# Modulation sums of a hybrid decoder block: two steps leave TensorE, four steps are joined in pairs

## The chip, the cores and the metric

The kernel runs on one core of one Trainium2 chip. The metric is the device time of one launch in microseconds (us), the median of three runs. The engines are named as the profile names them: PE is TensorE's stream of products (PEld its weight loads), DVE is VectorE, ACT is ScalarE, POOL is GpSimd, and SP is the queue that issues every DMA of this kernel.

## The reference

One decoder layer over 512 tokens of width 1024, all in float32. A conditioning vector c gives six modulation vectors; two of them (shift1 and scale1) shape the input of the token mixer, whose first product is one wide projection w_in:

```
c_act = jax.nn.silu(c)
mod = c_act @ w_ada[l] + b_ada[l]
shift1, scale1, gate1, shift2, scale2, gate2 = [m[:, None, :] for m in jnp.split(mod, 6, axis=-1)]
h = rms_norm(x, g_pre_mix[l]) * (1.0 + scale1) + shift1
y = token_mixer(h, ...)          # h @ w_in, then GLU and convolution, latent attention, gates
x = x + gate1 * rms_norm(y, g_post_mix[l])
h = rms_norm(x, g_pre_mlp[l]) * (1.0 + scale2) + shift2
y = jnp.square(jax.nn.relu(h @ w_mlp_in[l])) @ w_mlp_out[l]
x = x + gate2 * rms_norm(y, g_post_mlp[l])
```

In the mixer, the first 2048 columns of `h @ w_in` go through a GLU and a causal depthwise convolution of 31 taps over 1024 channels, the next 704 columns are the latents of the attention, and the last 2048 are gates.

## The kernel before

Every float32 product is made as three products of split operands: a matrix is split into a rounded high part (ACT casts it) and the rest (DVE subtracts), and PE adds high times high, high times low and low times high. So each weight that is loaded costs one ACT cast and one DVE subtraction before PE may use it. Tiles lie in two large SBUF arenas, `f_arena` (float32) and `r_arena` (the split parts), so nearly all operations carry one of these two names, and the line of a helper (L410) that issues them.

The kernel is written as a list of operations. A planner (class `Planner`) gives each one an estimated cost and a due time, and lays out the order of every engine's queue from them (`plan`, L327 on). It keeps a model of the DMA rings with one time at which they come free (`dma_free`, L341), and it repeats the plan up to 14 times with other places in the arenas and keeps the one that it reckons shortest. Engines then run their queues strictly in order. A change of any cost or of the list can therefore move work anywhere in the program.

The opening is the part that the change touches. The model width is cut in eight steps k of 128 channels. A step needs the shift and the scale of its 128 channels: `ada_load` brings 128 or more columns of w_ada (eight row blocks j, 4 DMAs of 256 KB for one step), `g1_load` brings 448 KB of w_in, and the sum over c's 1024 entries is made. `to_columns` (L657) turns the sums into columns, one channel to a partition, by products with `ones`, and adds the bias into the tile `mod`. `first_products` (L669) then makes the modulated h of the step (ACT writes the high part, DVE the low part), splits the step's w_in weights and issues 21 products of 128 x 512 into seven PSUM banks that collect all eight steps. In the prediction "the 168 products" are these 8 x 21.

How the sum over c is made depends on the step. For k = 0 and 1 (L689 to L713) PE makes it: 8 products of the column `cT` with the weights into one PSUM row, which ACT copies out. For k = 2 to 7 (L714 on, one step to a group of `KGRP`) DVE makes it on all partitions: one `tensor_scalar` and seven `scalar_tensor_tensor` on 256 columns, each reading the accumulator that the one ahead of it wrote, and the products with `ones` add up the partitions.

Ahead of the 168 products PE transposes the normalised x (32 transposes of 128 x 128); DVE and ACT copy them out. Behind them come the first GLU tiles, then the latent projection (its weights are the 128 x 704 splits on ACT and DVE), then the attention heads and, over a long stretch of DVE's queue, the convolution: 8 channel tiles with 31 steps of 128 x 512 each, 248 steps, two tiles in alternation. The convolution steps stand in DVE's queue between the splits and the softmax work that PE waits for.

Of the kernel before, what the change touches and what calls it, by code (L numbers as in the profile page):

```python
# [15 lines left out]
ALU = mybir.AluOpType  # L16

P = 128
# [3 lines left out]
KD = D // P  # L22
# [27 lines left out]
LEAD = 15000.0  # L50
SLOW = 4000.0
ADAS = (1, 1, 0, 4)
KGRP = ((2,), (3,), (4,), (5,), (6,), (7,))
HX, HA, HG, HC = 1.2e5, 1e5, 3e3, 1.1e5


# [113 lines left out]
class Planner:  # L170
# [154 lines left out]
    def plan(self):  # L325
        ops = self.ops
        pe_t = 0.0  # L327
        big = sum(o.cost for o in ops if o.eng == "pe") + TAIL
        for o in ops:
            o.dead = big  # L330
            if o.eng == "pe":
                pe_t += o.cost
                o.dead = pe_t
        for o in reversed(ops):
            lat = o.post + (2.0 * o.dma if o.dma else 0.0)
            for s in o.succ:
                q = ops[s]
                o.dead = min(o.dead, q.dead - q.cost - lat)
        heaps = {e: [] for e in self.NAMES}
        free = {e: 0.0 for e in self.NAMES}  # L340
        dma_free = 0.0  # L341
        landed = [0.0] * DEPTH
        future = []

        def key(o):
            return (o.rank, o.i) if o.eng == "pe" else (o.dead - o.hurry, o.i)

        for o in ops:
            o.ndep, o.ready = len(o.deps), 0.0
            if not o.ndep:  # L350
                heapq.heappush(future, (0.0, o.i))
        order = []
        now = 0.0
        while len(order) < len(ops):
            while future and future[0][0] <= now:
                o = ops[heapq.heappop(future)[1]]
                heapq.heappush(heaps[o.eng], (key(o), o.i))
            for e in self.NAMES:
                if free[e] <= now and heaps[e]:
                    o = ops[heapq.heappop(heaps[e])[1]]  # L360
                    o.t0 = now
                    free[e] = now + o.cost
                    if o.dma:
                        st = max(now + 1100.0, dma_free)
                        dma_free = st + o.dma
                        o.t1 = dma_free + 1100.0
                        landed.append(o.t1)
                        free[e] = max(free[e], landed[-DEPTH])
                    else:
                        o.t1 = free[e] + o.post  # L370
                    order.append(o)
                    for s in o.succ:
                        q = ops[s]
                        q.ndep -= 1
                        q.ready = max(q.ready, o.t1 if (q.eng != o.eng or o.dma) else free[e] if e == "pe" else max(free[e], o.t1 - 30))
                        if not q.ndep:
                            heapq.heappush(future, (q.ready, q.i))
            nxt = [free[e] for e in self.NAMES if free[e] > now and heaps[e]]
            if future:
                nxt.append(future[0][0])  # L380
            if not nxt:
                break
            now = max(now, min(nxt)) if min(nxt) > now else now
        assert len(order) == len(ops)
        self.length = max(o.t1 for o in ops)
        return order
# [28 lines left out]
def tile_hybrid_block(  # L415
# [34 lines left out]
    ones = const.tile([P, P], F32, name="ones")  # L450
# [13 lines left out]
    def emit(past, replay):  # L464
# [79 lines left out]
        def ada_load(ks):  # L544

            n = len(ks) * P
            b = fa.alloc(2 * KD * n)
            v = fa.v(b, "p (s j n) -> p s j n", j=KD, s=2)
            src = w_ada.rearrange("(j p) (s n) -> p s j n", p=P, s=6)
            step = KD // 2  # L550
            for j in range(0, KD, step):
                for s in range(2):
                    sp.dma_start(out=v[:, s, j:j + step], in_=src[:, s, j:j + step, ks[0] * P:ks[0] * P + n])
            return b, v
# [102 lines left out]
        def to_columns(src, lp, ks):  # L657

            for s in range(2):
                for i, k in enumerate(ks):  # L660
                    pe.matmul(pb.v(bg)[:, s * KD + k:s * KD + k + 1], lhsT=src[:, s, i * P:(i + 1) * P], rhs=ones[0:lp, 0:1],
                              start=True, stop=True)
            ksl = slice(ks[0], ks[-1] + 1)
            dve.tensor_tensor(mod[:, 0, ksl], pb.v(bg)[:, ksl], col("bada", ks[0], len(ks)), ALU.add)
            for k in ks:
                dve.scalar_tensor_tensor(mod[:, 1, k:k + 1], pb.v(bg)[:, KD + k:KD + k + 1], b1p[:, k:k + 1], col("gpm", k),
                                         op0=ALU.add, op1=ALU.mult)
# [17 lines left out]
                              stop=k == KD - 1 and wi == 1)  # L685
            w.free()


        plan.boost = 1000  # L689
        ad0 = [ada0]  # L690
        plan.hurry = HA - 1e4
        ad0.append(ada_load((1,)))
        wbs = []
        for k in range(2):
            plan.hurry = HA - (5e3 if k == 0 else 1.5e4)
            wbs.append(g1_load(k))
        plan.hurry = HG
        for k in range(2):
            av = ad0[k][1]
            ro = pb.v(bg)[0:1, 256:512].rearrange("p (s n) -> p s n", s=2)  # L700
            for j in range(KD):
                pe.matmul(ro, lhsT=cT[:, j:j + 1], rhs=av[:, :, j], start=j == 0, stop=j == KD - 1)
            fa.free(ad0[k][0])
            acc = fa.alloc(2 * P)
            accv = fa.v(acc, "p (s n) -> p s n", s=2)[0:1]
            act.copy(accv, ro)
            to_columns(accv, 1, (k,))
            fa.free(acc)
        plan.boost = 0
        plan.hurry = 0.0  # L710
        for k in range(2):
            first_products(k, wbs[k])

        for ks in KGRP:  # L714
            plan.hurry = HA - 1e4 * ks[0]
            n = len(ks) * P
            ab, av = ada_load(ks)
            ada_end = len(plan.ops) - 1
            plan.hurry -= 5e3
            wbs = [g1_load(k) for k in ks]  # L720
            plan.hurry = HG
            plan.boost = 1000
            acc = fa.alloc(2 * n)
            accv = fa.v(acc, "p (s n) -> p s n", s=2)
            for j in range(KD):
                if j == 0:
                    dve.tensor_scalar(accv, av[:, :, 0], cT[:, 0:1], None, ALU.mult)
                else:
                    dve.scalar_tensor_tensor(accv, av[:, :, j], cT[:, j:j + 1], accv, op0=ALU.mult, op1=ALU.add)
            fa.free(ab)  # L730
            to_columns(accv, P, ks)
            fa.free(acc)
            plan.boost = 0
            plan.hurry = 0.0
            for k, wb in zip(ks, wbs):
                first_products(k, wb)
# [1043 lines left out]
```

## Time and profile before

| what | time |
|---|---|
| median of three runs | 816.17 us (815.13 to 816.69) |
| the profiled execution | 815.82 us |
| its span, first to last instruction | 814.0 us |
| PE busy, DVE busy in the span | 796.5 us, 732.2 us |
| end of the 168 products | 66.2 us from the span's start |

The profiled execution lies 1.8 us above its own span and 0.35 us below the median. Times "at" a point are counted from the span's start. A busy PE in this profile is a modelled one, so stretches in which PE is all busy can hold short waits; the weight loads (PEld) show these better.

### The profile page before, as it was taken

Reading aid. Unit: us, or ns where it says so; the run is one execution under the profiler, and the core shown is the slowest. Engines: PE = TensorE matmul, PEld = TensorE weight load, DVE = VectorE, ACT = ScalarE, POOL = GpSimd, SP = SyncE. Lnnn points to the kernel's source line nnn. Section 1 sums busy time; section 2 is a strip of 40 time slices with the busy share of each in tenths; the row PEclk is TensorE's granted clock in tenths of the full one; section 3 lists DMA queues with packets and bytes.
Section 4 is the critical chain, followed back from the end, with each engine's and each line's share of the span. In section 5 each row is a group of like instructions: output and inputs, shape, how many; then the busy total and the mean of one; then the engine's idle time right before and its main releaser. Section 6 shows DMA issues by size and latency. Waiting matters only on the chain.

```text
span 814.0 us, 11293 instructions
## 1 busy us (share of the span) xinstructions
PE 796.5 (98%) x4222; PEld 681.1 (84%) x4222; DVE 732.2 (90%) x1049; ACT 441.6 (54%) x735; POOL 22.0 (3%) x77
## 2 busy tenths in 40 slices
PE   6999999999999999999999999999999999999996
PEld 3778988889897888878888889988998889888885
DVE  3898999999999999998899589899889989996696
ACT  5455453365885247237434387676665547554543
POOL 2001010000000000000000010000000000000001
PEclk9999999999999999999999999999999999999999
DMA  9989433112253250451799253026403580590302
GB/s 296 314 257 320 148 122 104 52 53 65 91 182 80 77 151 31 155 170 63 268 316 369 77 202 112 2 78 199 137 2 98 186 292 18 163 301 2 104 1 103
DMA packets 91337, 117.31 MB, mean 144 GB/s; under 512 B 7473, under 2 KB 66194, under 8 KB 91282
## 3 DMA queue, kind: packets, MB, share of 16 engines
q1 hardware_dynamic: 91282, 116.59, 44.9%
q8 instruction: 33, 0.54, 0.3%
q14 instruction: 22, 0.18, 0.1%
HBM read 108.18 MB, written 8.39 MB: 143 GB/s over the span
## 4 chain that ended last, share of the span: by engine, by line
PE 84%; DVE 8%; ACT 3%; DMA 2%; issue 1%; POOL 1%; SPq 0%; DVEq 0%
PE psum L410 84%; DVE f_arena L410 5%; DVE r_arena L410 3%; ACT f_arena L410 2%; ACT r_arena L410 1%; DMA c<-in_c_dram 1%; DMA f_arena<-in_w_in_dram 1%; POOL stats L410 1%; ACT stats L410 0%; SPq L410 0%; DMA rows<-in_kv_norm_g_dram 0%; DVE mod L410 0%; DVEq L1775 0%; DVEq L410 0%
## 5 line engine op out<-in xcount | busy, mean ns | idle before, releaser
L410 PE MATMUL psum<-r_arena 128*128 128x512 f32 (+3 forms) x3880 | 756.4, 355 | 0.9 <-ACT r_arena L410 0.6
L410 PEld LDWEIGHTS psum<-r_arena 128*128 128x128 f32 x3880 | 640.1, 189 | 100.7 <-ACT r_arena L410 2.6
L410 ACT CAST r_arena<-f_arena 128x1024 fp32r<-128x1024 f32 (+4 forms) x240 | 224.9, 964 | 169.1 <-PE psum L410 115.3
L410 DVE TENSOR_TENSOR r_arena<-f_arena,r_arena 128x1024 fp32r<-128x1024 f32 (+4 forms) x250 | 265.9, 1089 | 31.2 <-PE psum L410 21.4
L410 DVE SCALAR_TENSOR_TENSOR f_arena<-f_arena,cw 128x512 f32<-128x512 f32 x240 | 165.8, 738 | 0.0
L410 DVE TENSOR_TENSOR f_arena<-f_arena 128x1024 f32<-128x1024 f32 (+3 forms) x99 | 102.3, 1047 | 3.0 <-ACT r_arena L410 1.6
L410 ACT ACTIVATE f_arena<-f_arena 128x512 f32<-128x512 f32 (+4 forms) x112 | 66.1, 606 | 29.0 <-DVE f_arena L410 27.9
L410 ACT ACTIVATE f_arena<-psum 128x512 f32<-128x512 f32 x52 | 30.6, 594 | 71.9 <-PE psum L410 71.3
L410 DVE SCALAR_TENSOR_TENSOR f_arena<-f_arena,cT 128x256 f32<-128x256 f32 (+1 forms) x70 | 56.0, 801 | 7.4 <-DMA f_arena<-in_w_ada_dram 6.4
L410 DVE TENSOR_TENSOR f_arena<-psum,f_arena 128x512 f32<-128x512 f32 x64 | 42.9, 681 | 6.8 <-PE psum L410 6.8
L410 ACT COPY f_arena<-psum 128x512 f32<-128x512 f32 (+5 forms) x54 | 26.8, 517 | 33.2 <-PE psum L410 33.1
L410 PE MATMUL psum<-ident,f_arena 128*128 128x128 f32 x234 | 35.4, 291 | 8.2 <-DVE f_arena L410 8.1
L410 PEld LDWEIGHTS psum<-ident,f_arena 128*128 128x128 f32 x234 | 29.0, 149 | 14.1 <-DVE f_arena L410 9.3
L410 ACT CAST r_arena<-psum 128x512 fp32r<-128x512 f32 (+2 forms) x57 | 30.2, 563 | 12.1 <-PE psum L410 11.8
L410 DVE TENSOR_TENSOR r_arena<-psum,r_arena 128x512 fp32r<-128x512 f32 (+2 forms) x57 | 35.8, 654 | 0.6 <-ACT r_arena L410 0.3
L410 POOL TENSOR_TENSOR stats<-stats,nhalf 128x1 f32<-128x1 f32 (+1 forms) x17 | 13.3, 785 | 471.2 <-ACT stats L410 471.1
L410 ACT ACTIVATE r_arena<-f_arena 128x512 fp32r<-128x512 f32 (+3 forms) x20 | 13.0, 651 | 18.0 <-DVE f_arena L410 15.4
L410 ACT ACTIVATE r_arena<-f_arena,mod 128x512 fp32r<-128x512 f32 x8 | 6.5, 816 | 21.1 <-DVE mod L410 21.1
L410 DVE TENSOR_SCALAR f_arena<-f_arena,stats 128x1024 f32<-128x1024 f32 x8 | 6.0, 753 | 12.7 <-POOL stats L410 12.7
L410 DVE CUSTOM_DVE_ANT_0 f_arena<-psum,mask 128x128 f32<-128x128 f32 (+3 forms) x32 | 14.8, 481 | 0.1
L410 DVE SCALAR_TENSOR_TENSOR f_arena<-f_arena 128x512 f32<-128x512 f32 (+1 forms) x18 | 13.2, 740 | 0.0
L410 DVE SCALAR_TENSOR_TENSOR f_arena<-f_arena,psum 128x512 f32<-128x512 f32 x16 | 10.8, 678 | 2.2 <-ACT f_arena L410 2.2
(94 smaller groups left out, 182.9 us busy)
## 6 DMA issues: line engine op xcount, KB each, us to landing
f_arena<-in_w_ada_dram SPq DMA_DIRECT2D x16, 1024.0 KB
f_arena<-in_w_mlp_in_dram SPq DMA_DIRECT2D x32, 512.0 KB
f_arena<-in_w_mlp_out_dram SPq DMA_DIRECT2D x32, 512.0 KB
f_arena<-in_w_in_dram SPq DMA_DIRECT2D x24, 512.0 KB
f_arena<-in_w_ada_dram SPq DMA_DIRECT2D x32, 256.0 KB
f_arena<-in_x_dram SPq DMA_DIRECT2D x8, 512.0 KB
h_spill<-r_arena SPq DMA_DIRECT2D x16, 256.0 KB
f_arena<-in_w_attn_out_dram SPq DMA_DIRECT2D x8, 512.0 KB
```

The costliest lines, as they stand in the source:

```text
L410: getattr(self.real[o.eng], o.fn)(*o.a, **o.k)
```

## The change

- `KGRP` becomes `((0,), (1,), (2, 3), (4, 5), (6,), (7,))`: all eight steps go through the same loop, with steps 2 and 3 and steps 4 and 5 in one group each. A pair is loaded by 4 DMAs of 512 KB with rows of 1024 bytes (128 x 4 x 256), and summed by operations of 512 columns.
- The branch that made the sums of steps 0 and 1 on PE goes, with its two ACT copies.
- The sum on DVE has two accumulators, one for the even and one for the odd j: two `tensor_scalar` and six `scalar_tensor_tensor`, in alternation, so that an operation reads what the one before the last wrote.
- `to_columns` takes both accumulators: for each column of `mod` two products with `ones` that add up in PSUM, where there was one.
- The planner's DMA ring starts as free at 1500 in place of 0 (nanoseconds of its model).

```diff
-KGRP = ((2,), (3,), (4,), (5,), (6,), (7,))
+KGRP = ((0,), (1,), (2, 3), (4, 5), (6,), (7,))
...
-        dma_free = 0.0
+        dma_free = 1500.0
...
-                    pe.matmul(pb.v(bg)[:, s * KD + k:s * KD + k + 1], lhsT=src[:, s, i * P:(i + 1) * P], rhs=ones[0:lp, 0:1],
-                              start=True, stop=True)
+                    for q, a in enumerate(src):
+                        pe.matmul(pb.v(bg)[:, s * KD + k:s * KD + k + 1], lhsT=a[:, s, i * P:(i + 1) * P], rhs=ones[0:lp, 0:1],
+                                  start=q == 0, stop=q == len(src) - 1)
...
-        for k in range(2):
-            av = ad0[k][1]
-            ro = pb.v(bg)[0:1, 256:512].rearrange("p (s n) -> p s n", s=2)
-            for j in range(KD):
-                pe.matmul(ro, lhsT=cT[:, j:j + 1], rhs=av[:, :, j], start=j == 0, stop=j == KD - 1)
-            fa.free(ad0[k][0])
-            acc = fa.alloc(2 * P)
-            accv = fa.v(acc, "p (s n) -> p s n", s=2)[0:1]
-            act.copy(accv, ro)
-            to_columns(accv, 1, (k,))
-            fa.free(acc)
...
-            ab, av = ada_load(ks)
+            ab, av = ada0 if ks == (0,) else ada_load(ks)
...
-            acc = fa.alloc(2 * n)
-            accv = fa.v(acc, "p (s n) -> p s n", s=2)
+            acc = [fa.alloc(2 * n) for _ in range(2)]
+            accv = [fa.v(a, "p (s n) -> p s n", s=2) for a in acc]
             for j in range(KD):
-                if j == 0:
-                    dve.tensor_scalar(accv, av[:, :, 0], cT[:, 0:1], None, ALU.mult)
+                a = accv[j % 2]
+                if j < 2:
+                    dve.tensor_scalar(a, av[:, :, j], cT[:, j:j + 1], None, ALU.mult)
                 else:
-                    dve.scalar_tensor_tensor(accv, av[:, :, j], cT[:, j:j + 1], accv, op0=ALU.mult, op1=ALU.add)
+                    dve.scalar_tensor_tensor(a, av[:, :, j], cT[:, j:j + 1], a, op0=ALU.mult, op1=ALU.add)
```

The list of operations has changed, so the queues are planned anew. Three places follow, each as it stands before and after.

PE's queue in the opening, before. `ident` rows are transposes of x, `cT` rows the sums of steps 0 and 1, `ones` rows the products that make columns of `mod`, and r_arena rows the 168 products:

```order
L410 MATMUL psum<-f_arena,cT 1x256 x8
L410 MATMUL psum<-ident,f_arena 128x128 x6
L410 MATMUL psum<-ones,f_arena 128x1 x2
L410 MATMUL psum<-ident,f_arena 128x128
L410 MATMUL psum<-f_arena,cT 1x256 x8
L410 MATMUL psum<-r_arena 128x512 x3
L410 MATMUL psum<-ones,f_arena 128x1 x2
L410 MATMUL psum<-r_arena 128x512 x30
L410 MATMUL psum<-ones,f_arena 128x1 x2
L410 MATMUL psum<-r_arena 128x512 x23
L410 MATMUL psum<-ones,f_arena 128x1 x2
L410 MATMUL psum<-r_arena 128x512 x22
```

The same stretch of PE's queue after:

```order
L411 MATMUL psum<-ident,f_arena 128x128 x21
L411 MATMUL psum<-ones,f_arena 128x1 x4
L411 MATMUL psum<-r_arena 128x512 x7
L411 MATMUL psum<-ones,f_arena 128x1 x4
L411 MATMUL psum<-r_arena 128x512 x34
L411 MATMUL psum<-ones,f_arena 128x1
L411 MATMUL psum<-r_arena 128x512
L411 MATMUL psum<-ones,f_arena 128x1 x7
L411 MATMUL psum<-r_arena 128x512 x25
L411 MATMUL psum<-ones,f_arena 128x1
L411 MATMUL psum<-r_arena 128x512 x2
L411 MATMUL psum<-ones,f_arena 128x1 x7
```

The two blocks of eight cT products are gone, there are four `ones` products to a step instead of two, and the columns of step 1 now stand behind seven products of step 0 (before: three), those of the pair 2, 3 behind all but one of the products of steps 0 and 1.

DVE's queue at steps 0 to 2, before. A 128x512 COPY takes a transpose out of PSUM, `mod` rows finish a step's shift and scale (`cols_99` holds the bias and the gain as columns), r_arena rows are low parts (128x512 of h, 128x896 of w_in):

```order
L410 COPY f_arena<-psum 128x512 x3
L410 TENSOR_TENSOR mod<-psum,cols_99 128x1
L410 SCALAR_TENSOR_TENSOR mod<-psum,b1p,cols_99 128x1
L410 COPY f_arena<-psum 128x512
L410 TENSOR_SCALAR f_arena<-f_arena,mod 128x512
L410 TENSOR_TENSOR r_arena<-f_arena,r_arena 128x512
L410 TENSOR_TENSOR r_arena<-f_arena,r_arena 128x896 x2
L410 TENSOR_TENSOR mod<-psum,cols_99 128x1
L410 SCALAR_TENSOR_TENSOR mod<-psum,b1p,cols_99 128x1
L410 TENSOR_SCALAR f_arena<-f_arena,mod 128x512
L410 TENSOR_SCALAR f_arena<-f_arena,cT 128x256
L410 TENSOR_TENSOR r_arena<-f_arena,r_arena 128x512
```

The same place of DVE's queue after (a sum is two TENSOR_SCALAR and six SCALAR_TENSOR_TENSOR with cT):

```order
L411 SCALAR_TENSOR_TENSOR f_arena<-f_arena,cT 128x256 x6
L411 COPY f_arena<-psum 128x512 x2
L411 TENSOR_TENSOR mod<-psum,cols_99 128x1
L411 SCALAR_TENSOR_TENSOR mod<-psum,b1p,cols_99 128x1
L411 COPY f_arena<-psum 128x512
L411 TENSOR_SCALAR f_arena<-f_arena,mod 128x512
L411 COPY f_arena<-psum 128x512
L411 TENSOR_SCALAR f_arena<-f_arena,cT 128x256 x2
L411 SCALAR_TENSOR_TENSOR f_arena<-f_arena,cT 128x256 x6
L411 TENSOR_TENSOR r_arena<-f_arena,r_arena 128x512
L411 TENSOR_TENSOR r_arena<-f_arena,r_arena 128x896
L411 TENSOR_TENSOR mod<-psum,cols_99 128x1
```

The low part of step 0's h (the 128x512 subtraction) now stands behind the whole sum of step 1; before it followed its own scale at once.

DVE's queue at the end of the 168 products, before (128x704 rows are low parts of the latent projection's weights, the row that reads psum is the first GLU tile, and `pos4f` are the token positions):

```order
L410 TENSOR_TENSOR r_arena<-f_arena,r_arena 128x704 x2
L410 TENSOR_TENSOR r_arena<-f_arena,r_arena 128x512
L410 TENSOR_TENSOR r_arena<-f_arena,r_arena 128x704
L410 CAST pos4f<-pos_95 4x128
L410 SCALAR_TENSOR_TENSOR f_arena<-f_arena,psum 128x512
```

And after:

```order
L411 TENSOR_TENSOR r_arena<-f_arena,r_arena 128x512 x3
L411 TENSOR_TENSOR r_arena<-f_arena,r_arena 128x704 x3
L411 CAST pos4f<-pos_95 4x128
L411 TENSOR_TENSOR r_arena<-f_arena,r_arena 128x704 x4
L411 SCALAR_TENSOR_TENSOR f_arena<-f_arena,psum 128x512
```

Seven of the 128x704 splits stand ahead of the first GLU tile where three did. Further on in DVE's queue, 64 of the 248 convolution steps stand ahead of the first split of the normalised latents, where 60 did; ahead of the last attention heads' splits it is 134, where it was 129.

## Rows read from the trace of the kernel before

**Rows 1.** The page's first part: busy time of each engine, its share of the span and its instructions.

```profile
PE 796.5 (98%) x4222; PEld 681.1 (84%) x4222; DVE 732.2 (90%) x1049; ACT 441.6 (54%) x735; POOL 22.0 (3%) x77
```

**Rows 2.** Busy time of each engine by stretch (us from the span's start), then the granted PE clock, the DMA share and GB/s.

```profile
0.00:60.00 60.00, 52.07 (x241) 38.68 (x242) 42.82 (x93) 28.36 (x45) 6.66 (x56) 1.00 1.01 289
60.00:184.00 124.00, 123.92 (x678) 109.50 (x677) 120.55 (x207) 63.03 (x124) 5.58 (x8) 1.00 0.42 133
184.00:245.00 61.00, 60.50 (x393) 54.51 (x391) 60.69 (x149) 45.27 (x107) 0.00 (x0) 1.00 0.37 113
```

**Rows 3.** The chain that ended last, in order of time: start, length, what.

```profile
19.81 23.67 PE psum L410 x110
...
61.20 121.92 PE psum L410 x667
...
197.86 6.19 DVE f_arena L410 x14
...
245.29 118.00 PE psum L410 x534
```

**Rows 4.** Groups of instructions of one shape from 0 to 66 us: busy us, mean ns of one, idle time ahead of them.

```profile
L410 PE MATMUL psum<-r_arena 128*128 128x512 f32 x168 | 41.2, 398 | 0.1
...
L410 DVE SCALAR_TENSOR_TENSOR f_arena<-f_arena,cT 128x256 f32<-128x256 f32 x42 | 20.2, 482 | 0.9
...
L410 PE MATMUL psum<-f_arena,cT 128*1 128x256 f32 x32 | 7.4, 386 | 0.2 <-DVE mod L410 0.2
...
L410 PE MATMUL psum<-ones,f_arena 128*128 128x1 f32 x24 | 3.0, 229 | 0.0
```

**Rows 5.** PE and DVE in order of time in the opening: start, length, instructions merged into one row.

```profile
11.03 3.25 PE L410 MATMUL psum<-ident,f_arena 128*128 128x128 f32 x14
...
19.67 0.68 DVE L410 COPY f_arena<-psum 128x512 f32<-128x512 f32 x1
...
20.27 0.54 DVE L410 TENSOR_SCALAR f_arena<-f_arena,mod 128x512 f32<-128x512 f32 x1
...
23.36 0.96 PE L410 MATMUL psum<-r_arena 128*128 128x512 f32 x3
...
24.78 7.14 PE L410 MATMUL psum<-r_arena 128*128 128x512 f32 x30
```

**Rows 6.** DVE in order of time, steps 2 to 4: the sums and the low parts.

```profile
31.14 0.35 DVE L410 TENSOR_SCALAR f_arena<-f_arena,cT 128x256 f32<-128x256 f32 x1
31.52 0.49 DVE L410 SCALAR_TENSOR_TENSOR f_arena<-f_arena,cT 128x256 f32<-128x256 f32 x1
...
32.49 2.04 DVE L410 SCALAR_TENSOR_TENSOR f_arena<-f_arena,cT 128x256 f32<-128x256 f32 x4
34.45 0.69 DVE L410 TENSOR_TENSOR r_arena<-f_arena,r_arena 128x512 fp32r<-128x512 f32 x1
35.05 0.48 DVE L410 SCALAR_TENSOR_TENSOR f_arena<-f_arena,cT 128x256 f32<-128x256 f32 x1
35.44 1.08 DVE L410 TENSOR_TENSOR r_arena<-f_arena,r_arena 128x896 fp32r<-128x896 f32 x1
36.45 0.48 DVE L410 SCALAR_TENSOR_TENSOR f_arena<-f_arena,cT 128x256 f32<-128x256 f32 x1
```

**Rows 7.** Convolution steps on DVE in order of time; neighbours belong to two channel tiles, so an operation reads what the one before the last wrote.

```profile
80.38 0.54 DVE L410 TENSOR_SCALAR f_arena<-f_arena,cw,cols 128x512 f32<-128x512 f32 x1
80.83 1.41 DVE L410 SCALAR_TENSOR_TENSOR f_arena<-f_arena,cw 128x512 f32<-128x512 f32 x2
...
86.42 14.66 DVE L410 SCALAR_TENSOR_TENSOR f_arena<-f_arena,cw 128x512 f32<-128x512 f32 x22
```

**Rows 8.** PE's weight loads in order of time; a float32 product with `ones` shows as two loads.

```profile
37.25 0.64 PEld L410 LDWEIGHTS psum<-ones,f_arena 128*128 128x128 f32 x4
37.81 4.90 PEld L410 LDWEIGHTS psum<-r_arena 128*128 128x128 f32 x22
...
61.19 4.63 PEld L410 LDWEIGHTS psum<-r_arena 128*128 128x128 f32 x21 [0.51 <-ACT r_arena L410]
66.18 0.14 PEld L410 LDWEIGHTS psum<-ident,rows 37*128 37x128 f32 x1 [0.35 <-issue]
```

**Rows 9.** ACT in order of time: the high part of a step's h, with the idle time ahead of it and its releaser.

```profile
38.33 0.82 ACT L410 ACTIVATE r_arena<-f_arena,mod 128x512 fp32r<-128x512 f32 x1 [3.36 <-DVE mod L410]
```

**Rows 10.** Busy time by stretch as in rows 2, in tens of microseconds; the last number is what the DMA engines moved, in GB/s.

```profile
0.00:10.00 10.00, 2.26 (x10) 1.84 (x11) 1.70 (x4) 6.59 (x12) 4.46 (x47) 1.00 0.83 279
10.00:20.00 10.00, 9.81 (x47) 6.12 (x46) 4.19 (x11) 3.25 (x10) 1.51 (x3) 1.00 1.16 312
20.00:30.00 10.00, 10.00 (x46) 6.47 (x45) 8.34 (x16) 4.35 (x6) 0.12 (x1) 1.00 1.16 313
```

**Rows 11.** DVE in order of time from the end of the 168 products to the first convolution step.

```profile
60.21 3.23 DVE L410 TENSOR_TENSOR r_arena<-f_arena,r_arena 128x704 fp32r<-128x704 f32 x4
...
65.78 0.69 DVE L410 SCALAR_TENSOR_TENSOR f_arena<-f_arena,psum 128x512 f32<-128x512 f32 x1 [2.22 <-ACT f_arena L410]
...
68.19 2.68 DVE L410 TENSOR_TENSOR r_arena<-f_arena,r_arena 128x704 fp32r<-128x704 f32 x3
...
74.85 0.53 DVE L410 TENSOR_SCALAR f_arena<-f_arena,cw,cols 128x512 f32<-128x512 f32 x1
```

**Rows 12.** One group of PE's products of one shape from 66 to 183 us, as in rows 4.

```profile
L410 PE MATMUL psum<-r_arena 128*128 128x512 f32 x288 | 68.7, 393 | 0.0
```

More of the change, by code (lines that the diff above doesn't have):

```diff
@@ L686, in first_products @@
             w.free()
[L689 to L693, printed above, removed]
-        for k in range(2):
[L695 to L698, printed above, removed]
-            av = ad0[k][1]
-            ro = pb.v(bg)[0:1, 256:512].rearrange("p (s n) -> p s n", s=2)
-            for j in range(KD):
-                pe.matmul(ro, lhsT=cT[:, j:j + 1], rhs=av[:, :, j], start=j == 0, stop=j == KD - 1)
-            fa.free(ad0[k][0])
-            acc = fa.alloc(2 * P)
-            accv = fa.v(acc, "p (s n) -> p s n", s=2)[0:1]
-            act.copy(accv, ro)
-            to_columns(accv, 1, (k,))
-            fa.free(acc)
[L709 to L712, printed above, removed]
         for ks in KGRP:
@@ L722, in emit @@
             plan.boost = 1000
-            acc = fa.alloc(2 * n)
-            accv = fa.v(acc, "p (s n) -> p s n", s=2)
+            acc = [fa.alloc(2 * n) for _ in range(2)]
+            accv = [fa.v(a, "p (s n) -> p s n", s=2) for a in acc]
             for j in range(KD):
-                if j == 0:
-                    dve.tensor_scalar(accv, av[:, :, 0], cT[:, 0:1], None, ALU.mult)
+                a = accv[j % 2]
+                if j < 2:
+                    dve.tensor_scalar(a, av[:, :, j], cT[:, j:j + 1], None, ALU.mult)
                 else:
-                    dve.scalar_tensor_tensor(accv, av[:, :, j], cT[:, j:j + 1], accv, op0=ALU.mult, op1=ALU.add)
+                    dve.scalar_tensor_tensor(a, av[:, :, j], cT[:, j:j + 1], a, op0=ALU.mult, op1=ALU.add)
             fa.free(ab)
             to_columns(accv, P, ks)
-            fa.free(acc)
+            fa.free(*acc)
             plan.boost = 0
```

## The prediction

> **What bounds the kernel now.** I read the page's engine shares first: PE is busy for 98% of the span and DVE for 90% [rows 1]. So the question is not which engine is busy, but which one ends last in the stretch that the change touches. By stretches [rows 2] the reader should see that DVE is the freer engine only in the first 60 us (42.8 of 60 busy); from 60 to 184 it is busy for 120.6 of 124 us and from 184 to 245 for 60.7 of 61, beside a PE that shows no idle time either. The chain that ended last [rows 3] runs through PE at 19.8 to 43.5 and at 61.2 to 183, then in short pieces through DVE until 245, then through PE again. From 245 on PE sets the time, and the change moves little there. So what counts is how late PE and DVE are at 66, when the 168 products end, and at 245.
>
> In the opening I read PE's weight loads and DVE's rows side by side. At 61.19 a step's 21 products need 4.63 us, 0.2205 each [rows 8]. The columns of a step hold the loads for 0.56 us (37.25 to 37.81 for four loads, 0.14 each) [rows 8]. On DVE a sum operation that reads its predecessor starts 0.52 us after it ((2.04 - 0.48) / 3), while an operation that doesn't may start 0.39 us after it (35.05 to 35.44) [rows 6]. The two engines are near balance there, and the last step waits 0.51 us for ACT [rows 8].
>
> As a check of the method on the kernel before: at 24.78 three products are done [rows 5]; 165 x 0.2205 = 36.4, and six steps' columns 6 x 0.56 = 3.4, give 64.6; the trace has the end at 66.18 [rows 8]. The 1.6 us between are short waits.
>
> **The change part by part.** *Removed from PE:* the 32 instructions with cT, 7.4 us [rows 4], and two ACT copies. They stand ahead of and between the first products, so what they give back is an earlier start, and that has to be found by following the new queue.
>
> *Start of step 0.* 21 transposes from 11.03 at 3.25 / 14 = 0.232 [rows 5] end at 15.9. The sum of step 0 on DVE, 2 x 0.38 + 6 x 0.39 = 3.1 us (0.38 from 31.14 to 31.52) [rows 6], lies beside them. Eight loads for its columns, 1.1 us, then the two mod operations: 17.4. Its high part follows on ACT and seven products can run.
>
> *Step 1 ahead of step 0's low part.* DVE's queue now does an eviction, a scale, an eviction (0.60 + 0.54 + 0.60, spacing and length in [rows 5]) and then the whole sum of step 1, 3.1 us: 22.2. The products of step 0 with its low part, and all that PE has behind the columns of step 1, wait for that: the columns end at 23.4. So at 23.4 seven products are done, where before at 24.78 three were: a gain of 1.4 + 4 x 0.22 = 2.3 us.
>
> *The pair 2, 3.* From 22.2 DVE does two low parts, the mod work, and step 1's low parts: 0.60 + 1.01 + 0.2 + 1.01 + 0.54 + 0.60 [rows 5, 6] = 4.0, so 26.1. Its operations have 512 columns; the nearest rows are the alternating convolution steps, (14.66 - 0.75) / 21 = 0.66 and 0.45 for the first kind [rows 7], so 2 x 0.45 + 6 x 0.66 = 4.9: 31.0. Before, two single sums cost 2 x (0.38 + 7 x 0.52) = 8.0. PE has 34 products, 7.5 us, from 23.4: 30.9. It then makes the pair's columns, 16 loads and a product, 2.4 us, and waits for mod (0.4), for ACT (0.82 [rows 9]) and for a hand-over of 0.2: 34.8. Nothing else covers these 1.4 us.
>
> *The data:* the pair is complete after 7.2 MB, by the rates of 279, 312 and 313 GB/s at 24 us [rows 10], ahead of 26.1.
>
> *The rest.* 126 products, 27.8 us, and the columns of steps 4 to 7, 32 loads or 4.5 us, end at 67.1. The pair 4, 5 is summed by 40.9 where PE has work until 40.3; with that I take 67.5. **So the products end 1.3 us later** than at 66.2: the doubled columns cost 24 more loads for steps 2 to 7 (3.4 us), which takes more than the earlier start gives. Bounds: at 3.0 / 24 = 0.125 a product pass [rows 4] in place of 0.14 it is 0.7 less, and a second wait as long as that at the pair 2, 3 (1.4, less the 0.4 counted) makes it 1.0 more: +0.6 to +2.3.
>
> *DVE behind that.* Four of the 704-wide splits move ahead of the first GLU tile into time in which DVE waited (2.22 us at 65.78) or has become free. At 3.23 / 4 to 2.68 / 3 [rows 11] they are 3.4 us. The GLU tile comes 1.3 later, so the work from there to the first convolution step, at 74.85 before, is done 1.3 - 3.4 = 2.1 us earlier. But the new queue spends that: four more convolution steps stand ahead of the first latent split and five more ahead of the last heads', 2.65 and 3.3 us [rows 7]. DVE reaches these places 0.5 and 1.2 us later than before. Both engines are thus late by about the same, PE by 1.3 and DVE by 0.5 to 1.2.
>
> *A rule against the alternation.* Rows 6 show 0.39 between operations that are independent and 0.52 between dependent ones. The Trainium skill (VectorE: DVE Perf Modes, The DRAIN you can't avoid) says that the next operation doesn't start until the pipe is empty, with or without a semaphore, so that chaining is no matter. By it a single sum would still be 0.8 us longer than my 3.1. The rows speak against it here, and it is a rival below.
>
> *Elsewhere.* The new ring time of 1500 and the new list reorder the later queues in small pieces. From 245 PE is on the chain; I put nothing on this and 0.5 us on either side.
>
> **The sum:** 814.0 + 1.2 = 815.2 for the span, 817.0 for the profiled execution (1.8 around its span), and 817.4 against the median, which is 0.35 above that execution.
>
> **The rivals.**
> *Fast: DVE's lead counts.* The 288 products of 512 columns between 66 and 183 take 68.7 us, 0.2385 each, not 0.2205 [rows 12]: 5.2 us of waits are hidden in a PE that looks all busy. If PE there waits for DVE's low parts, PE's 1.3 vanish in them, and DVE's 2.1 come through where the added convolution steps fill gaps: 816.2 - 2.1 = 814.1. Against it: DVE shows no gaps [rows 2]. Its condition is that DVE's queue waits for PE somewhere before 245.
> *Absorbed:* these waits take up PE's delay and DVE brings nothing: 816.2.
> *Slow: the lead never arises.* If the latent weights land too late for seven splits ahead of the GLU tile, DVE saves nothing and still has the five convolution steps ahead of the heads, and the chain at 183 to 245 goes through DVE [rows 3]: +3.3, so 819.5. It decides if the seventh weight block lands after about 64. The first 30 us, at over 300 GB/s [rows 10], speak against it.
> *Slow: alternation brings nothing.* Then step 1's sum is 0.8 longer, and so is the last; the two pairs, at an operation's full length of 0.75 and the 0.04 that separate dependent ones (0.52 - 0.48) in place of 0.66, are also 0.8 longer. All four are waited for: +3.2 on my 1.2, so 820.6. The convolution rows and the 0.39 speak against it.
>
> **How the numbers follow.** Forecast 0.45, fast 0.22, absorbed 0.10, slow by DVE 0.18, slow by the chain 0.05. About 0.2% is what a measurement of this kernel can tell from no change: 814.5 and 817.8. The forecast's own range, 816.2 to 818.8 with the 0.5 for later queues, reaches over the upper line; I count a quarter of it (0.12) as slower. Faster 0.22; same 0.33 + 0.10 = 0.43; slower 0.12 + 0.18 + 0.05 = 0.35. The range goes from 813.8, just under the fast rival, to 819.8, just over the first slow one; it leaves out the last rival, part of the fast one that could give more, and some of the unknown in later queues.
>
> **What would show it.** Right: in the profile after, the 168 products end at 67 to 68; PE stands still at about 20 to 22 and for 1.4 us at 33; sums of 256 columns show a spacing near 0.39 and those of 512 near 0.66; eight loads stand ahead of each single step; the first convolution step comes by 73 and the PE stretch that starts at 245 before starts at 246 to 247. Wrong: products that end before 66 (then the columns are cheaper than two loads each, or step 0 starts earlier than I follow); a convolution that starts after 75 (the slow rival); a shorter stretch to 245 with the products late (the fast one); or a changed time behind 300 us, where I see no reason for any.

## The result

The changed kernel takes 817.64 us in the median of ten runs (815.73 to 819.71), the kernel before 815.37 in the same job (814.53 to 816.69, ten runs): ratio 1.0029, 95% interval 1.0020 to 1.0038. It is slower by 0.29%; the forecast was 817.4. A second job of ten runs gave 818.73 (815.26 to 819.95) and 1.0031 (1.0018 to 1.0044). Of the first ten runs five take 816.74 us or less and five 818.55 or more, so their median is the middle of a gap in which no run lies. The time agrees with the forecast, the way to it only in part: one term of the sum was 0.9 us too large, an instant in the opening 1.7 us too late, the time of one product too short, and a cost that the prediction doesn't name, PE's granted clock, made up the difference. In the last job below, one run of the kernel before took 993.8 us at a mean granted clock of 0.754, and the ratios leave it out.

The profiled execution of the changed kernel took 816.29 us with a span of 814.5. The page's busy times and the stretches of [rows 1] and [rows 2]:

```profile
PE 792.8 (97%) x4222; PEld 683.3 (84%) x4222; DVE 731.4 (90%) x1047; ACT 441.4 (54%) x733; POOL 24.9 (3%) x77
```

```profile
0.00:60.00 60.00, 48.44 (x239) 40.43 (x240) 47.03 (x99) 32.57 (x50) 7.12 (x56) 0.97 0.98 301
60.00:184.00 124.00, 123.92 (x678) 109.74 (x677) 118.75 (x202) 58.52 (x118) 5.70 (x8) 1.00 0.40 128
184.00:245.00 61.00, 60.68 (x394) 54.74 (x393) 60.62 (x146) 44.70 (x108) 0.00 (x0) 1.00 0.35 113
```

In the first 60 us PE is busy for 3.6 us less and DVE for 4.2 more, and the mean clock of that stretch is 0.97 in place of 1.00. The chain, as in [rows 3], leaves PE at 158, where it did at 183 before, goes through DVE and ACT from there to 245.5, and then through PE again as before:

```profile
20.46 12.21 PE psum L411 x57
33.88 124.07 PE psum L411 x650
245.55 115.06 PE psum L411 x523
496.99 301.83 PE psum L411 x1685
```

PE in order of time through the opening, to hold against [rows 5] and [rows 8]: start, length, merged instructions, idle time ahead with its releaser. The float32 product with `ones` shows as two records. The row of 37x37 stands directly behind the last of the 168 products, so its start is taken for their end, as at 66.18 before.

```profile
8.98 0.27 PE L411 MATMUL psum<-ident,c 8*128 8x8 f32 x1
...
10.51 3.54 PE L411 MATMUL psum<-ident,f_arena 128*128 128x128 f32 x21
14.21 1.13 PE L411 MATMUL psum<-ones,f_arena 128*128 128x1 f32 x8 [0.17 <-DVE f_arena L411]
16.82 1.88 PE L411 MATMUL psum<-r_arena 128*128 128x512 f32 x7 [1.47 <-ACT r_arena L411]
20.07 1.23 PE L411 MATMUL psum<-ones,f_arena 128*128 128x1 f32 x8 [1.37 <-DVE f_arena L411]
21.15 9.60 PE L411 MATMUL psum<-r_arena 128*128 128x512 f32 x34
...
33.88 5.96 PE L411 MATMUL psum<-r_arena 128*128 128x512 f32 x25 [1.22 <-ACT r_arena L411]
...
66.36 0.25 PE L411 MATMUL psum<-ident,rows 37*128 37x37 f32 x1
```

The reader is to see three places where PE stands still: 1.47 us ahead of 16.82, 1.37 ahead of 20.07 and 1.22 ahead of 33.88. Then see the 34 products at 21.15: 9.60 us, 0.28 each, where 0.2205 was expected. The stretches behind the first two waits say why (columns as in [rows 2]; the number behind POOL is the granted clock), first of the changed kernel, then of the kernel before:

```profile
16.00:18.00 2.00, 1.18 (x5) 1.01 (x6) 2.00 (x6) 0.77 (x1) 0.00 (x0) 1.00 1.07 357
18.00:20.00 2.00, 0.70 (x4) 0.23 (x2) 2.00 (x7) 0.94 (x1) 0.00 (x0) 1.00 1.10 349
...
22.00:24.00 2.00, 2.00 (x7) 1.60 (x6) 1.90 (x6) 0.82 (x1) 0.00 (x0) 0.60 1.09 360
24.00:26.00 2.00, 2.00 (x6) 1.53 (x5) 2.00 (x5) 0.58 (x1) 0.40 (x1) 0.55 1.06 376
```

```profile
16.00:18.00 2.00, 2.00 (x11) 0.64 (x9) 0.00 (x0) 0.00 (x0) 0.00 (x0) 1.00 1.10 343
18.00:20.00 2.00, 1.81 (x13) 1.33 (x13) 1.22 (x4) 1.49 (x4) 0.00 (x0) 1.00 1.20 292
...
22.00:24.00 2.00, 2.00 (x10) 0.87 (x8) 1.62 (x2) 0.69 (x2) 0.00 (x0) 1.00 1.16 311
24.00:26.00 2.00, 2.00 (x11) 1.54 (x10) 1.01 (x4) 0.72 (x2) 0.00 (x0) 1.00 1.20 297
```

PE was busy for 1.18 and 0.70 of 2 us, and then most of 22 to 26 was granted at 0.50, which is 1.2 of 2.4 GHz. Before, PE had the products with `cT` here, was busy for 2.00 and 1.81 of 2 us, and the clock stayed at 1.00. For the time of one product, a long run of PE's weight loads, to hold against the 21 loads of [rows 8]:

```profile
52.29 13.72 PEld L411 LDWEIGHTS psum<-r_arena 128*128 128x128 f32 x61
```

Forty loads more take 13.72 - 4.63 us, so a product is 0.227 us: the prediction's 0.2205 came from dividing the length of 21 loads, which holds 20 intervals and the last load, by 21.

DVE did what the change says. In order of time, to hold against [rows 6], [rows 7] and [rows 11]:

```profile
17.94 2.46 DVE L411 SCALAR_TENSOR_TENSOR f_arena<-f_arena,cT 128x256 f32<-128x256 f32 x6
...
25.17 4.06 DVE L411 SCALAR_TENSOR_TENSOR f_arena<-f_arena,cT 128x512 f32<-128x512 f32 x6
...
66.24 0.69 DVE L411 SCALAR_TENSOR_TENSOR f_arena<-f_arena,psum 128x512 f32<-128x512 f32 x1 [2.77 <-ACT f_arena L411]
...
70.51 0.54 DVE L411 TENSOR_SCALAR f_arena<-f_arena,cw,cols 128x512 f32<-128x512 f32 x1
```

The spacing is (2.46 - 0.48) / 5 = 0.40 at 256 columns and (4.06 - 0.75) / 5 = 0.66 at 512. The convolution starts 4.3 us earlier than before.

### The profile page after: what moved, and what is told of

Read it like the earlier page. It is cut to its first block, busy times and chain, and to the rows that moved or that the text cites. A ratio compares the mean times of both kernels' runs of the same rounds, so it can differ in the third digit from the quotient of the medians.

```text
span 814.5 us, 11278 instructions
## 1 busy us (share of the span) xinstructions
PE 792.8 (97%) x4222; PEld 683.3 (84%) x4222; DVE 731.4 (90%) x1047; ACT 441.4 (54%) x733; POOL 24.9 (3%) x77
## 4 chain that ended last, share of the span: by engine, by line
PE 81%; DVE 13%; ACT 3%; POOL 1%; issue 1%; DMA 0%; DVEq 0%; ACTq 0%
PE psum L411 81%; DVE f_arena L411 9%; DVE r_arena L411 5%; ACT f_arena L411 1%; ACT r_arena L411 1%; POOL stats L411 1%; DMA f_arena<-in_x_dram 0%; ACT stats L411 0%; DVEq L1753 0%; DVE mod L411 0%; DVEq L411 0%; DVE cT L411 0%; DVE cols L411 0%; ACTq L411 0%
## 5 line engine op out<-in xcount | busy, mean ns | idle before, releaser
L411 DVE SCALAR_TENSOR_TENSOR f_arena<-f_arena,cT 128x1024 f32<-128x1024 f32 (+2 forms) x64 | 53.7, 884 | 0.2
L411 ACT COPY f_arena<-psum 128x512 f32<-128x512 f32 (+4 forms) x52 | 26.2, 525 | 29.6 <-PE psum L411 29.6
L411 POOL TENSOR_TENSOR stats<-stats,nhalf 128x1 f32<-128x1 f32 (+1 forms) x17 | 15.4, 906 | 480.5 <-ACT stats L411 480.4
```

Source lines behind the costliest of these rows:

```text
L411: getattr(self.real[o.eng], o.fn)(*o.a, **o.k)
```

## The experiments

Theories: **path** (doubled columns and waits, as the prediction has it), **clock** (PE's clock falls after it has stood still; a "fall" is a stretch granted at 0.50), **later queues** (the new order behind 66 us). The ring time can be set aside without a run: with dma_free at 0 or at 1500, the kernel before and the changed kernel each have the same instructions in the same order on every engine. All runs stand in one table; a ratio is of the runs (not of the two medians) to the kernel before in the same job (medians of 815.37, 815.91, 815.58 and 815.44 us in the four jobs). Comments in the edits shown are notes for the reader. "End" is the end of the 168 products in the profiled execution, "rest" its span less that.

| kernel | median us (range) | ratio to before (95%) | mean clock of the runs | end | rest |
|---|---|---|---|---|---|
| before | 815.37 (814.53 to 816.69) | | 0.997 to 0.999 (later jobs) | 66.18 | 747.8 |
| changed | 817.64 (815.73 to 819.71) | 1.0029 (1.0020 to 1.0038) | 0.992 to 0.996 | 66.36 | 748.1 |
| again | 818.73 (815.26 to 819.95) | 1.0031 (1.0018 to 1.0044) | 0.990 to 0.995 | 69.34 | 748.4 |
| fill | 817.66 (815.76 to 818.36) | 1.0020 (1.0011 to 1.0029) | 0.994 to 0.998 | 67.83 | 748.1 |
| pe_open | 818.55 (817.97 to 818.79) | 1.0033 (1.0021 to 1.0045) | 0.997 to 0.998 | 68.01 | 748.5 |
| one_chain | 822.11 (819.32 to 822.65) | 1.0071 (1.0059 to 1.0084) | 0.987 to 0.994 | 72.37 | 747.9 |
| fill_both | 815.61 (814.71 to 816.14) | 1.0002 (0.9993 to 1.0010) | 0.997 to 0.998 | 65.41 | 748.3 |
| singles | 816.22 (815.24 to 818.62) | 1.0013 (1.0004 to 1.0023) | 0.992 to 0.996 | 68.10 | 748.5 |
| singles_join | 813.63 (812.08 to 814.57) | 0.9973 (0.9963 to 0.9982) | 0.991 to 0.995 | 64.97 | 747.8 |
| singles_join_fill | 812.54 (812.14 to 812.90) | 0.9959 (0.9946 to 0.9973) | 0.997 to 0.998 | 62.46 | 747.9 |
| pe_open_join | 814.81 (813.49 to 815.60) | 0.9988 (0.9979 to 0.9997) | 0.996 to 0.998 | 65.74 | 747.6 |
| join_pairs | 816.39 (814.05 to 817.12) | 1.0006 (0.9997 to 1.0015) | 0.990 to 0.995 | 67.02 | 748.3 |
| fill_act | 812.47 (811.70 to 812.75) | 0.9963 (0.9950 to 0.9975) | 0.997 to 0.999 | 61.66 | 749.0 |

The ends differ by 10.7 us, the rests by 1.4: what the products' end loses or gains goes one to one into the time, and what differs in the later queues stays within 1.4 us. That holds although the chain lies on DVE and ACT from 158 to 245: the first GLU tile, with which DVE goes on at 66.24, waits for these products too, by way of ACT.

**again**: the changed kernel, timed again.

> The changed kernel as it is, timed again. Three theories stand. Path: the doubled columns and the longer waits at the start of the steps make PE later, as the prediction has it; then the runs lie around 817.6 in one group. Clock: PE stands still longer at 14 to 20 us than before, its granted clock then falls to 0.50 (1.2 GHz) from 22.4 to 25.7 us, and the 34 products there take 9.6 us, not 7.5; some runs lose about 2.5 us more in the same way. Then the ten runs fall again into two groups, near 816.4 with a mean granted clock of 0.994 to 0.996 and near 819 with 0.992, and nothing between. Later queues: the difference comes from the new order behind 66 us; then the mean clock has nothing to do with the time.

There are the two groups, if with a wider spread. Of the twenty runs of both jobs, nine with a mean clock of 0.994 or more lie at 815.26 to 817.77, eleven with 0.992 or less at 818.36 to 819.95. This job's profile is one of the second kind (819.44 us, 0.992). PE in order of time, then three stretches:

```profile
20.81 1.87 PE L411 MATMUL psum<-ones,f_arena 128*128 128x1 f32 x8 [1.18 <-DVE f_arena L411]
22.54 9.56 PE L411 MATMUL psum<-r_arena 128*128 128x512 f32 x34
...
35.23 7.60 PE L411 MATMUL psum<-r_arena 128*128 128x512 f32 x25 [1.22 <-ACT r_arena L411]
...
69.34 0.25 PE L411 MATMUL psum<-ident,rows 37*128 37x37 f32 x1
```

```profile
18.00:20.00 2.00, 1.62 (x7) 0.83 (x5) 2.00 (x7) 0.94 (x1) 0.00 (x0) 0.77 1.09 350
20.00:22.00 2.00, 1.19 (x6) 1.20 (x6) 2.00 (x5) 0.00 (x1) 0.00 (x0) 0.50 1.11 349
...
36.00:38.00 2.00, 2.00 (x6) 1.51 (x5) 2.00 (x5) 2.00 (x3) 0.00 (x0) 0.54 1.17 275
```

The clock falls earlier here, ahead of step 1's columns (1.87 us, 1.23 in the other profile), and stays low from 19.1 to 25.9 us, against 22.4 to 25.8 there. It falls a second time behind the wait at 34, from 36.0 to 39.4, where the same 25 products take 7.60 us and not 5.96.

**fill**: products on PE into the first two waits, their results unused. The planner counts them at nothing (`plan.ops[-1].cost = 0.0`), so that the other instructions keep their places.

```diff
+            if ks == (0,):          # behind to_columns
+                for i in range(6):
+                    pe.matmul(pb.v(g1b[i])[:, 0:P], lhsT=ident, rhs=ident, start=True, stop=True)
...
+                if k == 0 and wi + hi == 0:     # behind the first seven products
+                    for i in range(11):
+                        pe.matmul(pb.v(bg)[:, 256:512], lhsT=w(0, 0, P)[0], rhs=hs(k)[0][:, 0:256], start=True, stop=True)
```

> The changed kernel, with 17 additional products on PE at the start (six of 128 columns around the columns of step 0, eleven of 256 columns behind the first seven products of step 0) whose results nobody uses; the order of all other work is the same on every engine. They lie in time in which PE stood still. Clock: the granted clock stays at 1.00 through 20 to 30 us, the 34 products take 7.5 to 7.8 us, the 168 products end near 64 to 65 and the time is 815.0 to 816.5, all runs within 1.5 us. Path: 34 products stay at 9.6 us or the time stays at 817.6. Later queues: the products may end earlier, but the time stays at 817.6.

```profile
14.73 1.46 PE L411 MATMUL psum<-ident 128*128 128x128 f32 x6
16.03 0.95 PE L411 MATMUL psum<-ones,f_arena 128*128 128x1 f32 x8
...
22.59 8.00 PE L411 MATMUL psum<-r_arena 128*128 128x512 f32 x34
...
33.77 7.54 PE L411 MATMUL psum<-r_arena 128*128 128x512 f32 x25 [1.27 <-ACT r_arena L411]
```

The first fall is gone (8.00 us), the second is there (7.54). In time the edit gave nothing in the median: three of the first six products (the six records at 14.73, two to a product) went ahead of step 0's columns, which came at 16.03, and nine of eleven runs have a clock of 0.994 to 0.996. The two with 0.998 took 815.76 and 816.19. The median, 817.66, is what I had put down for the other two theories. So as a test of the total it failed by its placing; as a test of the first fall it holds.

**fill_both**: the same idea behind the columns, and at the third wait too; no other instruction changes its place.

```diff
+            if ks == (0,):          # in to_columns, behind the products with ones
+                for i in range(7):
+                    pe.matmul(pb.v(g1b[0])[:, 0:P], lhsT=mask[:, 0:P], rhs=src[-1][:, 1, 0:P], start=True, stop=True)
+            if ks == (2, 3):        # zeros, added to a running sum
+                for i in range(6):
+                    pe.matmul(pb.v(g1b[0])[:, 0:P], lhsT=mask[:, 0:P], rhs=src[-1][:, 1, 0:P], start=False, stop=False)
```

> The changed kernel with products on PE whose results nobody uses, in three places where PE stood still: seven of 128 columns behind the columns of step 0, eleven of 256 columns behind the first seven products, six of 128 columns (by a matrix of zeros, added to a running sum) behind the columns of the pair 2, 3. All other work keeps its order. Clock: the granted clock stays at 1.00 from 14 to 60 us in every run; the first fall cost 9.6 - 7.6 = 2.0 us (the 34 products) and the second 7.6 - 6.0 = 1.6 us (the 25 behind the pair), so the 168 products end at 64.4 to 65 and the time is 814.1 to 815.0, in one group. Path: what the products gain is lost again in a longer wait for the pair's sum, and the time stays at 816 to 817.6. Later queues: 817.6.

```profile
11.01 4.08 PE L411 MATMUL psum<-ident,f_arena 128*128 128x128 f32 x21
...
21.74 7.98 PE L411 MATMUL psum<-r_arena 128*128 128x512 f32 x34
29.56 0.28 PE L411 MATMUL psum<-ones,f_arena 128*128 128x1 f32 x2
...
32.92 5.98 PE L411 MATMUL psum<-r_arena 128*128 128x512 f32 x25
...
65.41 0.25 PE L411 MATMUL psum<-ident,rows 37*128 37x37 f32 x1
```

All eleven runs have 0.997 or 0.998, and they lie within 1.4 us. The time, 815.61, is that of the kernel before (815.58 in this job). It is less of a gain than the 814.1 to 815.0 that I expected. Still it decides between the theories: more work on PE, in the same order, takes away what the change had added. The products behind the first fall lose 9.60 - 7.98 = 1.6 us, those behind the second 7.60 - 5.98 = 1.6.

**pe_open**: steps 0 and 1 summed on PE again, the rest as changed.

```diff
-KGRP = ((0,), (1,), (2, 3), (4, 5), (6,), (7,))
+KGRP = ((2, 3), (4, 5), (6,), (7,))
...
+                pe.matmul(ro, lhsT=cT[:, j:j + 1], rhs=av[:, :, j], start=j == 0, stop=j == KD - 1)
```

> The sums of steps 0 and 1 back on PE, as in the kernel before; steps 2 to 7 as in the changed kernel, in two chains with pairs (the two accumulators of a step lie in one buffer). Clock: PE has the 16 instructions with cT again, its clock does not fall in the opening, and the time is 815.0 to 816.5 in one group. Path: the earlier start of 2.3 us is lost and the doubled columns stay, so it is slower than the changed kernel: 817.6 + 2.3 = 819.9. Later queues: 817.6, since steps 2 to 7 set the new order.

```profile
24.30 7.82 PE L411 MATMUL psum<-r_arena 128*128 128x512 f32 x33
...
68.01 0.25 PE L411 MATMUL psum<-ident,rows 37*128 37x37 f32 x1
```

No fall, as the clock theory wants, and yet 818.55, 2.0 above what I gave that theory and 1.4 below the path's 819.9: the path theory's part is real too. Steps 2 to 7 in this form cost 2.6 us against before (815.91 in this job), and moving steps 0 and 1 to DVE gives back 818.55 - 815.61 = 2.9 where no fall comes with it (the kernel before was 0.3 slower in this job than in that of fill_both, so 2.6 to 2.9).

**one_chain**: one accumulator, one load for a column.

```diff
-            acc = [fa.alloc(2 * n) for _ in range(2)]
+            acc = [fa.alloc(2 * n)]
```

> The changed kernel with one accumulator for a step: each sum is one chain, and each column takes one load, not two. Path: 32 loads fewer, 4.5 us at 0.14 each, against sums that are about 0.8 us longer at steps 0 and 1 and at the pair 2, 3, all waited for: 817.6 - 4.5 + 2.4 = 815.5. Clock: PE stands still longer in the opening, so the fall stays or comes earlier and both groups of times stay: 816 to 820. Later queues: 817 to 818.

```profile
21.00 0.98 PE L411 MATMUL psum<-ones,f_arena 128*128 128x1 f32 x4 [5.97 <-DVE f_arena L411]
...
72.37 0.25 PE L411 MATMUL psum<-ident,rows 37*128 37x37 f32 x1
```

Slowest of all, though PE has 32 loads less: PE stood still for 5.97 us in one piece, the profile shows two falls of 17 us together between 16 and 46 us, and five of six runs have a mean clock of 0.987. The path's 815.5 was wrong by 6.6, and the time lies above what I gave the clock theory as well.

**singles** and **singles_join**: steps 2 to 5 one by one; then also one load for a column.

```diff
-KGRP = ((0,), (1,), (2, 3), (4, 5), (6,), (7,))
+KGRP = ((0,), (1,), (2,), (3,), (4,), (5,), (6,), (7,))
...
+            if ks[0] >= 2:          # singles_join only
+                dve.tensor_tensor(accv[1], accv[0], accv[1], ALU.add)
+                accv = accv[1:]
             to_columns(accv, P, ks)
```

> The changed kernel with steps 2 to 5 one by one, two chains and two loads for each column as before. Path: the doubled columns stay, the 1.2 us wait behind the pair's 16 loads goes: 817.6 - 1.2 = 816.4. Clock: the standing still in the opening stays and with it the first fall, but the second fall (36 to 39 us, behind the pair's wait) is gone, so one group only, with a mean clock of 0.996, at 815.1 to 816.3. Rival: DVE, which is full from 20 to 32 us, needs 1.3 us more for two single sums than for the pair and PE waits for it: 817 to 819.

> As singles, and from step 2 on the two accumulators are added on DVE, so that each column takes one load. Path: 24 loads fewer than singles, 24 x 0.14 = 3.4 us: 816.2 - 3.4 = 812.8, faster than both kernels. Clock: the first fall stays (2.0 us are still lost). Rival: six additions of about 0.3 us and two single sums make DVE late between 20 and 40 us, PE waits for it and the time stays at 815 to 817.

First two rows of singles, with eight loads and 21 products from one to the other, then singles_join, with four loads and 21 products from its first row to its third:

```profile
39.55 0.28 PE L411 MATMUL psum<-ones,f_arena 128*128 128x1 f32 x2
...
45.24 0.28 PE L411 MATMUL psum<-ones,f_arena 128*128 128x1 f32 x2
```

```profile
51.62 0.50 PE L411 MATMUL psum<-ones,f_arena 128*128 128x1 f32 x4
51.99 5.07 PE L411 MATMUL psum<-r_arena 128*128 128x512 f32 x21
56.89 0.50 PE L411 MATMUL psum<-ones,f_arena 128*128 128x1 f32 x4
...
64.97 0.25 PE L411 MATMUL psum<-ident,rows 37*128 37x37 f32 x1
```

Without pairs there is no wait behind them, yet singles does not fall into one group: its clocks go from 0.992 to 0.996. Its profile (0.993) has one fall, but a longer one than the changed kernel's: the granted clock is under 1.00 in every stretch from 20 to 28 us. The additions bring 816.22 - 813.63 = 2.6 us. These rows size the doubled columns: from one step's columns to the next are 45.24 - 39.55 = 5.69 us with eight loads and 56.89 - 51.62 = 5.27 with four, both with 21 products. Four loads more cost 0.42, so a load more is 0.105 us, not 0.14, and 24 of them are 2.5 us.

**singles_join_fill**: as singles_join, with the first two groups of products of fill_both.

> As singles_join, with the first two groups of unused products of fill_both, so that PE does not stand still in the opening. Clock: no fall, 2.0 us less than singles_join: about 810.8, and a mean clock of 0.998. Path: the same time as singles_join, because the wait for the sums on DVE takes the place of the slow products.

```profile
21.52 5.01 PE L411 MATMUL psum<-r_arena 128*128 128x512 f32 x21
27.32 0.61 PE L411 MATMUL psum<-ones,f_arena 128*128 128x1 f32 x4 [0.79 <-DVE f_arena L411]
...
62.46 0.25 PE L411 MATMUL psum<-ident,rows 37*128 37x37 f32 x1
```

812.54 in one group, at 0.997 and 0.998: 0.4% faster than the kernel before. Against singles_join it gains 1.1 and not 2.0 us. PE, now ahead, waits 0.79 for the sum of step 2, a wait that the profile of singles_join doesn't have: a part of what the clock gives back is taken by the next wait, as the path theory said.

**pe_open_join**: as singles_join, with steps 0 and 1 on PE.

> The sums of steps 0 and 1 on PE as in the kernel before; steps 2 to 7 one by one, in two chains that are added on DVE, with one load for a column. It differs from singles_join only in who sums steps 0 and 1, and from the kernel before only in the two chains with their addition. Path: PE sets the time there and has the same work as before, so the shorter sums bring nothing: 815.3 to 816.0. Rival: the shorter sums on DVE make PE's short waits of 1.6 us in the opening go, and it is at 814.

814.81, between both expectations: the shorter sums bring 0.6 us by themselves. Three of its eleven runs have a mean clock of 0.996, at 815.22 to 815.60; where they lost it, no profile shows. Its distance to singles_join_fill, 2.3 us, is again what moving steps 0 and 1 is worth with PE kept busy.

**join_pairs**: the changed kernel with the addition (the edit of singles_join, pairs kept).

> The changed kernel with its pairs, and from step 2 on the two accumulators are added on DVE, so that each column takes one load. Path: 24 loads fewer, which by singles against singles_join is worth 2.6 to 3.1 us: 817.6 - 2.8 = 814.8. But the pair's sum ends 0.6 us later by the addition, and what PE waits for there grows: up to 815.4. Clock: the waits in the opening and behind the pair stay, so two groups of times 2 to 3 us apart stay too, with mean clocks near 0.995 and 0.992.

816.39, two groups (814.05 to 815.12 at 0.994 and 0.995; 815.86 to 817.12 at 0.993 and less) with medians 1.9 us apart, and the time 1.0 to 1.6 us above that expected.

**fill_act**: as singles_join_fill, with `VDVE = 0`.

> As singles_join_fill, and the scaling for the low part of steps 0 and 1 is on ACT, not on DVE, which is full from 20 to 40 us while ACT is busy for about half of it. Path: step 1's sum starts 0.5 us earlier and step 2's sum, for which PE waited 0.8 us at 26.5, about 1 us: 812.5 - 0.8 = 811.7. Rival: the low part of step 0 now waits for ACT behind the high parts, PE waits for it, and the time stays at 812.5 or is worse.

The end came 0.8 us earlier (61.66), the time did not (812.47): no difference that can be measured.

## Why the prediction came out

- **What the products' end loses goes into the time, one to one**: right. The rest is 747.6 to 749.0 in thirteen profiles.
- **The start of the opening's products**: 1.7 us too late. In fill_both, whose transposes start at 11.01 as in the forecast (11.03) and whose clock doesn't fall, the 34 products start at 21.74; the forecast was 23.4. About half is the 21 transposes: 4.08 us there and 3.54 in the changed kernel, not 4.87, which came from a row of before with 14 of them. So the gain over the kernel before is 24.78 - 21.74 + 4 x 0.227 = 3.9 us and not 2.3. A part is lost again in the wait at the pair, which is only 0.20 in pe_open: in the time, moving steps 0 and 1 is worth 2.6 to 2.9 and 2.3 by two pairs of runs without a fall.
- **24 more loads, 3.4 us**: this term was mis-sized. They cost 2.5 by the rows of singles and singles_join, and 2.6 by the medians of these two and of pe_open against the kernel before. My lower bound, 0.125 a pass, was still too high.
- **0.2205 us a product**: too short, 0.227 is right: 1.1 us over the 165 products of the check on the kernel before. So most of the 1.6 us that the check lacked were not short waits. The walk through the changed kernel lacks the same, and I held its end, 67.5, against the measured 66.18, not against the check's 64.6. With the 1.6 us added, the same working would have given 819.0. By the same token the hidden waits of the fast rival are 288 x (0.2385 - 0.227) = 3.3 us, not 5.2.
- **The 1.4 us wait at the pair**: right, 1.22 at 32.7 to 33.9 (forecast 33.4 to 34.8).
- **"PE has 34 products, 7.5 us"**: this step failed. It took one time for a product for granted behind a wait, at 20 to 22, that I had forecast myself. With the fall they took 9.60, without it 7.98. Without falls the end is at 65.41 in fill_both, 2.1 us before the forecast 67.5 and 0.8 before that of the kernel before. The falls took that back and more: 815.6 without any, 816.65 in the median of the nine runs of the changed kernel with the higher clock, 819.3 in that of the eleven with the lower. The end of 67 to 68 that I had named as a sign of being right was in neither profile: 66.36 in one, 69.34 in the other. (The two profiles, at 0.996 and 0.992, show what a run of each group can look like, not that all are alike: the clock is low for 3.4 us in one and for 10.2 in the other, and five of the nine runs have 0.994, which lies between.)
- **DVE 0.5 to 1.2 us late at the latent and heads splits**: not seen. Seven splits stand ahead of the GLU tile, the convolution starts at 70.51 (forecast: by 73), DVE reaches the first split of the normalised latents at 127.08 (before: 127.24), and the stretch to 245 ends at 245.55 (forecast 246 to 247).
- **Rivals**: the fast one fell, since DVE's 4.3 us of lead leave the rest at 748.1. The slow one by the latent weights did not come. The dearest, that alternation brings nothing, fell by the spacing of 0.40 against 0.52 in [rows 6]. The Trainium skill (VectorE: DVE Perf Modes, The DRAIN you can't avoid) says that the next operation doesn't start until the pipe is empty, and also that one that is not held starts earlier; the first is not borne out here between operations of the two chains, which start 0.40 apart at a length of 0.48. What the rival would have cost was under-estimated: a single chain is at 822.1, 32 loads fewer included, with 17 us at the lower clock in its profile.

So 817.4 was right by luck, by errors of opposite sign: without falls it should have read 815.6, 1.8 less, and the falls add 2.2 and 2.8 in the medians of the two jobs, each against the kernel before in its job. Why an execution has one fall or more stays open. The executions differ in when the first data land (PE's product with `c` starts at 8.79 to 10.32 in these profiles), but no run here tells which of them gets the second fall.

## What to carry to other kernels

A wait on TensorE can cost more than its length. Here waits of 1.2 to 1.5 us were followed by products at half the clock in some executions and not in others, so when an edit moves work off TensorE and it stands still more often, cost the products after the wait at both levels. If the median sits between two heaps of runs, sort the runs by their mean granted clock before explaining the median. Two alternating chains on VectorE were worth having here, where the sum is waited for (0.6 us by pe_open_join), but the two halves are better added there (2.6 us by singles and singles_join) than by a second load on the engine that sets the time. And when a walk through a queue comes out short on the kernel before, add that shortfall to the walk through the changed one.

## What was not expected of the hardware

- Waits of 1.47 and 1.37 us with seven products between them were followed by a granted clock of 0.50; the same waits filled with unused products by 1.00 in the profile of fill_both, whose eleven runs all have a mean clock of 0.997 or 0.998, as the kernel before has.
- The same program had one fall in one profile and two in another. The Trainium skill (TensorE: Matmul & The Clock Gate, Part 1: The HAM clock gate) says of the slow products at the start of a kernel that their number varies from run to run. In these traces it is so in the middle of the opening: the 25 products took 5.96 us in one execution and 7.60 in the other.
- An additional load with one column of output costs 0.105 us between products, where the weight loads of the kernel before had suggested 0.14.
